# A two-layer encoder trunk: the Winograd steps of its MLPs in pairs that share operand quads, and a part of the QKV stage ordered by hand

## The chip, the core and the metric

One NeuronCore of a Trainium2 chip computes the whole trunk in one launch. Its engines run beside each other and wait for one another by semaphores: TensorE (PE) multiplies, VectorE (DVE), ScalarE (ACT) and GpSimd (POOL) work element by element, and transfers are issued from queues, here mostly those of SyncE (SP) and ScalarE. The metric is the device time of one execution in microseconds (us), lower is better.

## The reference

Everything is float32, 1024 tokens of width 1024. Layer 0 is a gated recurrent block, layer 1 chunked attention on keys and values that are computed once from layer 0's output. Each layer ends in an MLP of width 4096, and the change lies there and in the stage behind the first one:

```python
def sqrelu_mlp(hn, w1, w2):
    return jnp.square(jax.nn.relu(hn @ w1)) @ w2

def reference(...):
    for layer in range(DEPTH):          # DEPTH = 2
        ...                             # mixer of the layer, h = h + g1 * y
        hn = modulate(rms_norm(h, norm2_g[layer]), sh2, sc2)
        h = h + g2[:, None, :] * sqrelu_mlp(hn, mlp_w1[layer], mlp_w2[layer])
        if layer == N_A_LAYERS - 1:
            k_pad, v_pad = shared_kv(h, c_act, kv_norm_g, kv_ada_w, kv_ada_b, kv_w, k_norm_g)
    return h
```

Layer 1 begins with its own query projection from a norm of `h`, then the projection of the shared keys and values: the QKV stage.

## The kernel before

**Precision.** Every float32 operand is split into a high part (a rounding copy on ScalarE, L196) and a low part (what is left, a subtraction on VectorE, L200). `mm3` (L329 to L331) multiplies high by high, high by low and low by high: three matmuls, 128 by 128 by 512 columns, for each block product.

**Two products by Winograd's scheme.** Both matrix products of an MLP run in steps. A step takes a quad, two by two blocks of weights, and makes the four results with seven block products instead of eight (`PROD` lists them with their operand names B11, T1, T2, B22, B21, T3, T4 and the PSUM bank that each goes to). A block product is four times `mm3`, 12 matmuls. The sums of weight blocks are formed by four adds (`add_quad`, L126), those of the activations by four subtractions (L632 for the MLP's input, L1202 for the hidden layer). Banks are accumulated on: product 2 goes to the bank that product 0 began, 3 to that of 1, and 5 and 6 to that of 2, and after each product an engine reads what the bank holds into its place (`read`). So the next product on a bank must wait for the read of the one before. `Quads.step` runs products 0 to 5 of a step, with the last product (6) of the step before it between its second and third one (`late`).

**The first product** makes blocks p = 0 to 15 of the hidden layer: 0 and 1 by plain products, 2 to 15 by steps. ScalarE copies products 0 to 2 out of their banks (L1282), VectorE adds products 3 to 5 (L1284), ScalarE squares the positive part (L1213, L1214). `store` writes eight blocks for each p to `hid` in DRAM from ScalarE's queue: the four results first, then, when the sums are made, the four sums.

**The second product** makes steps s = 0 to 15 (layer 0: 0 to 14, and the last two output blocks by plain products on the extra weights `w2t`, so that the next norm can begin). Step s multiplies the quad of output blocks of s mod 4 with hidden blocks s to s+3, a window that moves on by one block each step; blocks 16 to 18 are 0 to 2 again, which the layout of `w2` allows for. Seven operand halves are therefore loaded and split for each step (`hid_item`, tile `ws`, split tiles `s`), but the first step needs four blocks at once, 28 operand tiles. VectorE adds each product from its bank to `h` (L1306), which `reload` brings back from the spilled copy `hsp` (L1271).

**The planner.** `Stream` holds one list of loads. Its clock `now` advances by one with each block product. After a product it issues what it may: loads up to `ns` raw tiles in flight (`load`, L159), splits up to a limit of live operands for weights (`w`, 8) and activations (`a`, `cap`), the quad sums (`p`) and the adaLN reductions (`u`, L362: rows of the modulation weights times the conditioning vector). Low parts are held back in `los` and flushed after the next product. All of layer 0 and the MLP of layer 1 stand in the order in which the code emits them (`manual_schedule`); the QKV stage and the attention are ordered by a scheduler. In the first product the quad sums go to VectorE, in the second, from step 2 on, to GpSimd (`G if s > 1 else V`).

## Time and profile before

| | before |
|---|---|
| median of 3 runs | 2332.1 us (2330.79 to 2334.56) |
| the profiled execution | 2332.22 us, span 2330.4 us, mean granted clock 0.994 |
| TensorE busy | 2248.5 us, 96% |
| VectorE, ScalarE, GpSimd busy | 1742.8, 1243.6 and 425.3 us |
| moved by DMA | 363.32 MB |
| layer 0's mixer; its MLP; QKV; attention; output projection and layer 1's MLP | about 0 to 480; to 1100; to 1370; to 1615; to 2330 us |

How to read the profile: a row of a group of instructions gives the line of the code, engine, operation, tiles written and read, sizes and count, then the busy time and mean duration in ns of one, then the idle time before them and what ended it. A row of the order of time gives start, duration, engine and the idle time just before in square brackets with the instruction that ended it. A row of a stretch gives the busy time of each engine in it, the clock granted to TensorE (1.00 is full speed), the mean busy share of the DMA engines and the rate. Matmuls overlap: of 512 columns each shows some 390 ns, while the next one starts earlier.

### The profile page before, as it was taken

What the parts mean: (1) busy time and instruction counts of PE and PEld (TensorE: products, weight loads), DVE (VectorE), ACT (ScalarE), POOL (GpSimd) and SP (SyncE); (2) the same over time, 40 slices, a digit from 0 to 9 for tenths busy, and PEclk for the clock granted to TensorE, in tenths of its full rate; (3) what the DMA queues carried; (4) which work ended last, traced back from release to release, by engine and by line L of the source; (5) the groups of instructions that cost most, each with busy time, mean ns of one, the idle gap of its engine ahead of it and who ended that gap; (6) DMA issues with size and microseconds to landing.
All of it is one profiled execution on the core that took longest, in us unless ns stands there. A gap on an engine that the chain in (4) does not pass through costs nothing. (4 is left out here: it accounts for less than half of the span.)

```text
span 2330.4 us, 29543 instructions
## 1 busy us (share of the span) xinstructions
PE 2248.5 (96%) x10588; PEld 1866.4 (80%) x10588; DVE 1742.8 (75%) x2560; ACT 1243.6 (53%) x2148; POOL 425.3 (18%) x439
## 2 busy tenths in 40 slices
PE   4999999999999899999999999999999999899999
PEld 2878878778888678888888889997888888678887
DVE  8579889698777887777777649995485556877775
ACT  5587793374555633344443259994375555633342
POOL 0001010200000033331000248863100000033332
PEclk9999999999999999999999999999999999999999
DMA  8225457426666855555344200024124444854444
GB/s 318 73 70 155 134 184 274 157 89 237 250 255 249 318 197 159 150 166 186 107 129 135 86 10 10 10 62 149 62 72 170 170 170 173 302 205 152 150 147 142
DMA packets 141631, 363.32 MB, mean 156 GB/s; under 512 B 14924, under 2 KB 17100, under 8 KB 141484
## 3 DMA queue, kind: packets, MB, share of 16 engines
q1 hardware_dynamic: 113756, 278.45, 35.4%
q10 hardware_dynamic: 23824, 71.44, 8.3%
q0 software_dynamic: 3904, 11.54, 1.9%
q8 instruction: 83, 1.36, 0.2%
q14 instruction: 64, 0.52, 0.1%
HBM read 260.19 MB, written 89.65 MB: 150 GB/s over the span
## 5 line engine op out<-in xcount | busy, mean ns | idle before, releaser
L329 PE MATMUL b<-s,wh 128*128 128x512 f32 (+1 forms) x2532 | 996.0, 393 | 22.8 <-DVE s L1306 7.0
L330 PE MATMUL b<-s,wh 128*128 128x512 f32 (+1 forms) x2532 | 992.3, 392 | 8.7 <-DVE s L825 5.3
L331 PE MATMUL b<-s,wl 128*128 128x512 f32 x2296 | 900.0, 392 | 8.8 <-DVE wl L200 8.8
L329 PEld LDWEIGHTS b<-s,wh 128*128 128x128 f32 (+1 forms) x2532 | 476.7, 188 | 132.3 <-ACT wh L196 9.1
L330 PEld LDWEIGHTS b<-s,wh 128*128 128x128 f32 (+1 forms) x2532 | 476.8, 188 | 115.5 <-DVE s L825 6.3
L196 ACT ACTIVATE wh<-ws 128x1024 fp32r<-128x1024 f32 (+3 forms) x302 | 291.6, 975 | 486.0 <-POOL ws L126 277.9
L331 PEld LDWEIGHTS b<-s,wl 128*128 128x128 f32 x2296 | 432.5, 188 | 103.4 <-DVE wl L200 10.5
L200 DVE TENSOR_TENSOR wl<-ws,wh 128x1024 fp32r<-128x1024 f32 (+1 forms) x249 | 305.3, 1228 | 86.5 <-ACT wh L196 82.7
L1306 DVE SCALAR_TENSOR_TENSOR s<-b,mod,s 128x512 f32<-128x512 f32 x221 | 164.9, 746 | 112.5 <-PE b L331 111.9
L200 DVE TENSOR_TENSOR s<-ws,s 128x512 fp32r<-128x512 f32 x284 | 221.3, 796 | 6.6 <-ACT s L196 6.6
L196 ACT ACTIVATE s<-ws 128x512 fp32r<-128x512 f32 x284 | 165.0, 618 | 76.9 <-DMA ws<-hid 39.1
L126 POOL TENSOR_TENSOR ws<-ws 128x512 f32<-128x512 f32 x21 | 28.7, 1368 | 954.7 <-DVE s L1306 375.3
L330 PE MATMUL b<-wl,s 128*128 128x512 f32 x384 | 149.9, 390 | 0.0
L329 PE MATMUL b<-wh,s 128*128 128x512 f32 x384 | 149.0, 389 | 0.0
L331 PE MATMUL b<-wh,s 128*128 128x512 f32 x384 | 146.5, 389 | 1.1 <-DVE s L593 1.1
L1284 DVE TENSOR_TENSOR s<-s,b 128x512 f32<-128x512 f32 x84 | 57.3, 684 | 107.5 <-PE b L331 96.2
L1282 ACT ACTIVATE s<-b 128x512 f32<-128x512 f32 x84 | 50.0, 595 | 92.5 <-PE b L331 92.4
L362 DVE CUSTOM_DVE_ANT_0 ws<-ws,cb,vec 128x1024 f32<-128x1024 f32 x59 | 75.0, 1278 | 31.7 <-DMA ws<-in_ada_dram 25.2
L331 PE MATMUL b<-s,wh 128*128 128x512 f32 x236 | 91.8, 389 | 0.0
L335 DVE TENSOR_TENSOR s<-b,s 128x384 fp32r<-128x384 f32 x144 | 82.6, 593 | 11.1 <-ACT s L334 10.6
L1598 POOL TENSOR_SCALAR s<-s,sm 128x640 f32<-128x640 f32 (+4 forms) x128 | 86.0, 684 | 22.4 <-DVE sm L1596 19.4
L1593 ACT ACTIVATE s<-s,sm 128x640 f32<-128x640 f32 (+4 forms) x128 | 88.3, 696 | 0.7 <-DVE sm L1591 0.7
(166 smaller groups left out, 2990.6 us busy)
## 6 DMA issues: line engine op xcount, KB each, us to landing
hid<-s ACTq DMA_DIRECT2D x128, 512.0 KB, 4.8
ws<-hid SPq DMA_DIRECT2D x118, 512.0 KB, 4.7
ws<-in_w_dram SPq DMA_DIRECT2D x220, 256.0 KB, 3.5
ws<-in_ada_dram SPq DMA_DIRECT2D x56, 512.0 KB, 4.6
s<-in_ada_dram SPq DMA_DIRECT2D x40, 512.0 KB, 8.2
ws<-in_w_in_dram SPq DMA_DIRECT2D x22, 512.0 KB, 7.4
hsp<-s SPq DMA_DIRECT2D x32, 256.0 KB, 2.0
s<-hsp SPq DMA_DIRECT2D x16, 512.0 KB, 7.2
```

The costliest lines, as they stand in the source:

```text
L196: self.nc.scalar.activation(out=hi[:rows, :n], in_=src, func=AF.Copy)
L200: self.nc.vector.tensor_tensor(out=lo[:rows, :n], in0=src, in1=hi[:rows, :n].bitcast(F32), op=ALU.subtract)
L329: PE.matmul(ps, ah, bh, start=start, stop=False, skip_group_check=more)
L330: PE.matmul(ps, ah, bl, start=False, stop=False, skip_group_check=more)
L331: return PE.matmul(ps, al, bh, start=False, stop=stop, skip_group_check=more).ins
L335: V.tensor_tensor(out=lo, in0=src, in1=hi.bitcast(F32), op=ALU.subtract)
L362: V.tensor_tensor_reduce(out=t, in0=t, in1=cb, op0=ALU.mult, op1=ALU.add, scale=1.0, scalar=bias, accum_out=dst)
L1282: A_.activation(out=t, in_=ps, func=AF.Copy)
L1284: V.tensor_tensor(out=t, in0=t, in1=ps, op=ALU.add)
L1306: V.scalar_tensor_tensor(out=t, in0=ps, scalar=g2[:, m : m + 1], in1=t, op0=ALU.mult, op1=ALU.add)
L1593: A_.activation(out=p[:, lo:640], in_=p[:, lo:640], func=AF.Exp, scale=-1.0, bias=m, accum_out=s1)
L1598: G.tensor_scalar(out=p[:, lo:640], in0=p[:, lo:640], scalar1=sm[:, 4 + e : 5 + e], scalar2=1.0, op0=ALU.mult, op1=ALU.mult)
```

## The change

1. `Quads.pair` runs two steps together: products 0 and 1 of the first, 0 and 1 of the second, 2 and 3 of each, 4 and 5 of each, then 6 of the first; 6 of the second waits for the next pair. Blocks 14 and 15 of the first product run so, and all steps of the second (layer 0's last, 14, alone).
2. In the second product steps 2t and 2t+1 share hidden blocks 2t to 2t+3. The window moves by two blocks every two steps; block 18 falls away. The weight layout follows (`w2`, `w2t`), and the planner's weight queue is interleaved (`interleave`).
3. Numbers of the planner: `ns` 10, then 11 raw tiles; `cap` for activations up to 24, growing from block 14 and 15's pair on; `strict`, by which all held-back low parts are emitted ahead of a quad sum on VectorE; another spread of the adaLN loads; other delays for the stores of blocks 12 to 15.
4. The quad sums of the second product are all on VectorE.
5. `store` writes the block that only layer 0's plain products use (B12) for p = 0, 1, 14, 15 of layer 0 alone, else 256 KB instead of 512 in that transfer.
6. The hand-set order ends later: the first group of the query projection is inside it, with `late_head` placing the second half's norm.

```diff
@@ Stream
+    def interleave(self, n):
+        q = self.queue["w"]
+        a, b = q[-n : -n // 2], q[-n // 2 :]
+        q[-n:] = [x for two in zip(a, b) for x in two]
@@ Stream.step
         if it["use"]:
+            if it["raw"] is None and self.strict and it["mine"]:
+                los, self.los = self.los, []
+                for low in los:
+                    low[2]()
@@ mlp_units
-            ada_late(0 if l or q == 2 else 2 if q in (3, 15) else 3)
-        for s in STEPS[: 16 if l else 15]:
-            def quad(s):
-                c = slice(s * 128, s * 128 + 512)
-                ws.add_quad(*(I["w2"][l][s % 4][x][:, c] for x in range(4)), 512,
-                            G if s > 1 else V)
...
+            ada_late(0 if l or q in (2, 14, 15) else 2 if q == 3 else 4 if q < 9 else 3)
+        ws.interleave(8)
+        def quad(s):
+            c = slice(s // 2 * 256, s // 2 * 256 + 512)
+            ws.add_quad(*(I["w2"][l][s % 4][x][:, c] for x in range(4)), 512, V)
+
+        def quads(t):
+            for s in range(2 * t, 2 * t + (2 if l or t < 7 else 1)):
+                quad(s)
+            if l or t < 7:
+                ws.interleave(8)
+
+        for nm in NAMES:
+            hid_item(l, [(0, nm), (1, nm)])
+            hid_item(l, [(2, nm), (3, nm)])
+            if nm == "B11":
+                quads(0)
+        for t in range(7):
+            for n, nm in enumerate(NAMES):
+                if n == 4:
+                    quads(t + 1)
+                hid_item(l, [(2 * t + 4, nm), (2 * t + 5, nm)])
@@ Quads
+        def pair(self, *two):
+            two = [(a[0], [bank(), bank(), None], *a[1:]) for a in two]
+            for x in (0, 2, 4):
+                for n, a in enumerate(two):
+                    if x == 4:
+                        a[1][2] = bank()
+                    self.product(x, *a)
+                    self.product(x + 1, *a)
+                    if x == 0 and n == 0:
+                        self.end()
+            self.product(6, *two[0])
+            self.late = two[1]
@@ mlp_body
-                nc.scalar.dma_start(hid[p][:, 0:8:7], ca.rearrange(f, a=2))
+                if l == 0 and p in (0, 1, 14, 15):
+                    nc.scalar.dma_start(hid[p][:, 0:8:7], ca.rearrange(f, a=2))
+                else:
+                    nc.scalar.dma_start(hid[p][:, 0:1], ca[:, hs(0)].unsqueeze(1))
...
-            for d, job in zip((2, 4, 13) if p == 14 else (6, 8, 13) if p == 15 else (2, 4, 8),
+            for d, job in zip({12: (2, 3, 4), 13: (2, 3, 4), 14: (2, 16, 20), 15: (6, 18, 22)}.get(p, (2, 4, 8)),
...
+        ws.strict = True
         quads = Quads()
-        for p in range(2, 16):
+        def hidden(p):
...
-                    ws.cap["a"] = 4 * x + 4
-                    if x == 3:
-                        reload(0, 1)
+                    ws.cap["a"] = min(24, 4 * x + 4)
+                    ws.ns = 10
+                    if x in (3, 5):
+                        reload(x - 3, x - 2)
+            return [ws.next() for _ in range(4)], 4, nrm.op, read, after
+
+        for p in range(2, 14):
+            quads.step(*hidden(p))
+        quads.pair(hidden(14), hidden(15))
...
+        for t in range(8):
+            if l or t < 7:
+                quads.pair(second(2 * t), second(2 * t + 1))
+            else:
+                quads.step(*second(2 * t))
@@ QKV
-    tokens(qt, n3, 0, 0, lambda k: head(k, n3))
+    def late_head(k):
+        if k == 1:
+            n3.mm(1)
+        elif k == 4:
+            n3.bc(1)
+            n3.mod(1, (0, 1, 2, 3))
+        elif k == 6:
+            n3.mod(1, (4, 5, 6, 7))
+
+    tokens(qt, n3, 0, 0, late_head)
+    order.close()
```

**How the order moves, at three places.** First SyncE's queue at layer 0's seam, where the first product ends and the second begins. `in_w_dram` stands for both weights, `hid` are operand loads, `hsp` the reload of `h`. Before, from the first operand load on:

```order
L159 DMA ws_5523<-hid 128x2x512
L159 DMA ws_5568<-hid 128x2x512
L159 DMA ws_5572<-in_w_dram 128x512
L159 DMA ws_5662<-in_w_dram 128x512
L159 DMA ws_5702<-in_w_dram 128x512 x2
L159 DMA ws_5707<-hid 128x2x512
L159 DMA ws_5735<-hid 128x2x512
L159 DMA ws_5741<-hid 128x2x512
L159 DMA ws_5769<-hid 128x2x512
```

After, from the same place:

```order
L163 DMA ws_5548<-hid 128x2x512
L163 DMA ws_5571<-hid 128x2x512
L163 DMA ws_5613<-in_w_dram 128x512
L163 DMA s_5648<-in_w_dram 128x512
L163 DMA s_5650<-in_w_dram 128x512 x2
L163 DMA s_5653<-in_w_dram 128x512
L163 DMA ws_5664<-in_w_dram 128x512
L163 DMA ws_5688<-in_w_dram 128x512 x2
L163 DMA ws_5734<-hid 128x2x512
L163 DMA ws_5738<-hid 128x2x512
L1293 DMA s_5770<-hsp_2446 128x1024
```

Two quads of weights instead of one are now loaded behind the first name's operands, some of them into tiles outside the ring `ws`, and the reload of `h` comes sooner, ahead of most operands.

Second the quad sums late in layer 1's second product. On GpSimd before, steps 13 and 14:

```order
L126 TENSOR_TENSOR ws_18791<-ws_18851 128x512
L126 TENSOR_TENSOR ws_18817<-ws_18851,ws_18791 128x512
L126 TENSOR_TENSOR ws_18795<-ws_18817,ws_18851 128x512
L126 TENSOR_TENSOR ws_18795<-ws_18817,ws_18795 128x512
L126 TENSOR_TENSOR ws_18943<-ws_19004 128x512
L126 TENSOR_TENSOR ws_18970<-ws_19004,ws_18943 128x512
```

On VectorE after, between bank reads (L1335), low parts (L208) and two sets of sums (L123) for the pair of steps 12 and 13:

```order
L208 TENSOR_TENSOR s_18612<-ws_18406,s_18612 128x512
L123 TENSOR_TENSOR ws_18505<-s_18552 128x512
L123 TENSOR_TENSOR ws_18530<-s_18552,ws_18505 128x512
L123 TENSOR_TENSOR ws_18509<-ws_18530,s_18552 128x512
L123 TENSOR_TENSOR ws_18509<-ws_18530,ws_18509 128x512
L1335 SCALAR_TENSOR_TENSOR s_17074<-b_18647,mod_83,s_17074 128x512
L208 TENSOR_TENSOR wl_18637<-ws_18505,wh_18636 128x1024
L208 TENSOR_TENSOR s_18639<-s_18429,s_18639 128x512
L208 TENSOR_TENSOR s_18643<-s_18429,s_18643 128x512
L1335 SCALAR_TENSOR_TENSOR s_17076<-b_18451,mod_83,s_17076 128x512
L1335 SCALAR_TENSOR_TENSOR s_17123<-b_18677,mod_83,s_17123 128x512
L123 TENSOR_TENSOR s_18557<-ws_18614 128x512
```

GpSimd has no sums left in the MLPs; on VectorE a set of four stands in one piece among the bank reads.

Third TensorE at the very end, before: the last rows of product 5 and the first of product 6, both on bank `b_19245`.

```order
L329 MATMUL b_19245<-s_19241,wh_19238 128x512
L330 MATMUL b_19245<-s_19241,wh_19238 128x512
L331 MATMUL b_19245<-s_19241,wl_19239 128x512
L329 MATMUL b_19245<-s_18815,wh_19243 128x512
L330 MATMUL b_19245<-s_18815,wh_19243 128x512
L331 MATMUL b_19245<-s_18815,wh_19243 128x512
```

After: the last rows of product 6 of the pair's first step, whose twelve matmuls are all on `b_19047`, and the first of the second step's product 6 on `b_19049`.

```order
L337 MATMUL b_19047<-s_19125,wh_19174 128x512
L338 MATMUL b_19047<-s_19125,wh_19174 128x512
L339 MATMUL b_19047<-s_19125,wh_19174 128x512
L337 MATMUL b_19049<-s_18848,wh_19176 128x512
L338 MATMUL b_19049<-s_18848,wh_19176 128x512
L339 MATMUL b_19049<-s_18848,wh_19176 128x512
```

A whole product now stands between the last two that go to one bank.

56 lines of the change are left out of this document (22 added, 34 removed).

## The prediction

> **What bounds the kernel now.** I read the page's busy times first, then the 60 us stretches of the whole span, then TensorE's own order of time where a stretch fell short, and last what the other engines and the queues did there. The page: engine, busy us, share of the span, instructions.
>
> ```profile
> PE 2248.5 (96%) x10588; PEld 1866.4 (80%) x10588; DVE 1742.8 (75%) x2560; ACT 1243.6 (53%) x2148; POOL 425.3 (18%) x439
> ```
>
> TensorE is the bound: the change can only win what TensorE stands idle or runs slowly. Stretches of 60 us (PE, PEld, DVE, ACT, POOL busy with instruction counts, then granted clock, DMA share, GB/s):
>
> ```profile
> 720.00:780.00 60.00, 60.00 (x266) 49.70 (x265) 48.10 (x70) 36.39 (x59) 0.00 (x0) 1.00 0.71 255
> 780.00:840.00 60.00, 50.34 (x205) 39.95 (x204) 51.29 (x70) 28.07 (x46) 6.57 (x4) 0.94 0.85 302
> 1920.00:1980.00 60.00, 60.00 (x267) 49.69 (x266) 34.92 (x47) 32.44 (x48) 0.00 (x0) 1.00 0.50 183
> 1980.00:2040.00 60.00, 51.98 (x216) 41.65 (x215) 51.36 (x75) 38.56 (x65) 0.00 (x0) 0.94 0.86 302
> 2040.00:2100.00 60.00, 57.31 (x246) 46.94 (x245) 48.48 (x57) 21.00 (x31) 18.78 (x12) 0.97 0.57 196
> 2100.00:2160.00 60.00, 60.00 (x267) 49.69 (x266) 46.00 (x58) 21.94 (x33) 19.01 (x12) 1.00 0.53 161
> ```
>
> Full stretches hold 266 matmuls of 512 columns, one per 0.2256 us, so a product of 12 takes 2.71 us and a step of seven 19.0. The three short stretches are the seams between the first and the second product, in layer 0 (780 on) and layer 1 (1980 on). TensorE's idle times there, the first three rows and 827.50 in layer 0, the next five in layer 1, then one after layer 0's last step; the row of waits is for 2065 to the end:
>
> ```profile
> 786.35 0.47 PE L329 MATMUL b<-s,wh 128*128 128x512 f32 x1 [2.78 <-DVE s L1306]
> 800.55 0.50 PE L329 MATMUL b<-s,wh 128*128 128x512 f32 x1 [2.79 <-ACT wh L196]
> 803.32 0.80 PE L331 MATMUL b<-s,wl 128*128 128x512 f32 x1 [2.03 <-DVE wl L200]
> ...
> 827.50 0.50 PE L331 MATMUL b<-s,wl 128*128 128x512 f32 x1 [2.03 <-DVE wl L200]
> 2011.83 0.47 PE L329 MATMUL b<-s,wh 128*128 128x512 f32 x1 [2.22 <-DVE s L1306]
> 2014.98 0.47 PE L329 MATMUL b<-s,wh 128*128 128x512 f32 x1 [0.17 <-DVE s L1306]
> 2026.98 0.50 PE L329 MATMUL b<-s,wh 128*128 128x512 f32 x1 [3.59 <-ACT wh L196]
> 2029.75 0.80 PE L331 MATMUL b<-s,wl 128*128 128x512 f32 x1 [2.03 <-DVE wl L200]
> 2054.11 0.50 PE L331 MATMUL b<-s,wl 128*128 128x512 f32 x1 [2.69 <-DVE wl L200]
> 1075.83 0.47 PE L329 MATMUL b<-s,wh 128*128 128x512 f32 x1 [0.94 <-DVE s L1306]
> 1128.89 1.21 PE L331 MATMUL b<-wh,s 128*128 128x512 f32 x4 [1.10 <-DVE s L593]
> PE b L329 <- DVE s L1306: 0.9, 1, 0.9
> ```
>
> The seams' waits are 2.78+2.79+2.03+2.03 = 9.63 us in layer 0 and 2.22+0.17+3.59+2.03+2.69 = 10.70 in layer 1. The releasers are splits of weights and adds on VectorE, but these were late themselves; stretches of 5 us show why (the same columns, DMA share and GB/s last):
>
> ```profile
> 780.00:785.00 5.00, 3.57 (x16) 2.63 (x14) 4.90 (x9) 3.11 (x7) 0.00 (x0) 1.00 1.02 387
> 785.00:790.00 5.00, 3.62 (x15) 2.77 (x16) 5.00 (x8) 4.35 (x8) 0.00 (x0) 1.00 1.05 388
> 790.00:795.00 5.00, 5.00 (x24) 4.14 (x23) 5.00 (x9) 4.94 (x10) 0.00 (x0) 1.00 1.03 388
> ...
> 800.00:805.00 5.00, 2.42 (x6) 1.70 (x7) 4.93 (x8) 4.52 (x8) 0.00 (x0) 0.75 0.75 288
> 805.00:810.00 5.00, 5.00 (x14) 3.92 (x14) 3.27 (x5) 0.59 (x2) 0.00 (x0) 0.56 1.02 328
> 810.00:815.00 5.00, 5.00 (x24) 4.13 (x23) 3.25 (x6) 1.79 (x3) 0.00 (x0) 1.00 1.04 399
> 2025.00:2030.00 5.00, 0.98 (x3) 0.55 (x4) 4.78 (x7) 3.65 (x5) 0.00 (x0) 0.79 0.71 260
> 2030.00:2035.00 5.00, 5.00 (x13) 3.94 (x14) 3.27 (x5) 2.02 (x4) 0.00 (x0) 0.53 1.00 321
> 2055.00:2060.00 5.00, 5.00 (x17) 3.93 (x16) 4.15 (x6) 1.63 (x3) 0.00 (x0) 0.66 0.91 309
> ```
>
> Two things are to be seen: the DMA engines are full at 387 to 399 GB/s while VectorE is full too, and behind a pair of waits TensorE computes at about half clock. That half clock costs, as busy time times the missing share, 2.42x0.25 + 5x0.44 = 2.81 us in layer 0 and 0.98x0.21 + 5x0.47 + 5x0.34 = 4.26 in layer 1.
>
> **The change, part by part.** All sums are made against the profiled execution, 2332.2 us beside a span of 2330.4; the median of the three runs, 2332.1, is the same number.
>
> (1) TensorE's work: the same 10,238 rows of matmuls. Cost 0.
>
> (2) The seams. Counted from the planner, product by product: before, the eight products ahead of the second product carry 12.06 MB of loads and stores, 554 GB/s over 8x2.71 us, against 399 that the row shows. The 28 operand tiles of one quad set (four blocks, seven names) are used up in seven products. Now 14 products share them, and the last 11 products ahead of the second product with its first three carry 15.2 MB (layer 0: 15.5) in 14x2.71 = 37.9 us, 401 to 408 GB/s: still full, but the transfers needed last are used 14 products after the seam, not seven. The slack tells more than the rate: before, a weight's VectorE split stands two to five products ahead of its first use and a hid operand's four to five; now four to six and five to nine. One product of slack is 2.71 us and the longest wait above is 3.59. A second bank effect goes with it: a PSUM bank is read by VectorE (L1306) and accumulated on again; a step leaves two products between these, a pair at least two and mostly three or four, which covers the 2.78 and 2.22. So I cost the seams at no wait: -9.63 -10.70, and with them the half clock, -2.81 -4.26. The cover is this slack; if it is gone, the next thing late is the split of the second weight of pair (0,1) or a hid operand behind ScalarE, which now queues eight half-tile splits at a time behind loads. Bounds: nothing is left, or all of it stays; the row nearest to one left wait is 2.03 to 2.79 us plus 1.7 to 2.8 of half clock, so 4 to 5.5 each. I take none.
>
> The half clock's length has a second source. The Trainium skill, "TensorE: Matmul & The Clock Gate", Part 1, says that an idle window of about 3.4 us halves the clock and some 3.4 us of work restores it. By that, as an estimate, three such stretches would cost 3x1.7 = 5.1 us and the forecast would be 2.0 us higher; the rows show half clock after waits of 2.69 us and for more than 5 us, and they decide.
>
> (3) The sums of w2's quads go from GpSimd to VectorE, 108 instructions. Rows of VectorE's hid splits in the second product (2100 to 2280 us) and at layer 1's seam (1985 to 2065, hardly any GpSimd beside them), of its adds in the first product (1740 to 1980), of GpSimd's adds (2100 to 2280), and of the adaLN reductions (the page); the number behind the comma is ns of one:
>
> ```profile
> L200 DVE TENSOR_TENSOR s<-ws,s 128x512 fp32r<-128x512 f32 x65 | 56.1, 863 | 0.0
> L200 DVE TENSOR_TENSOR s<-ws,s 128x512 fp32r<-128x512 f32 x43 | 27.8, 683 | 2.8 <-ACT s L196 2.8
> L126 DVE TENSOR_TENSOR ws<-ws,ws 128x512 f32<-128x512 f32 x39 | 26.9, 690 | 0.9
> L126 POOL TENSOR_TENSOR ws<-ws,ws 128x512 f32<-128x512 f32 x17 | 26.6, 1567 | 0.8
> L362 DVE CUSTOM_DVE_ANT_0 ws<-ws,cb,vec 128x1024 f32<-128x1024 f32 x59 | 75.0, 1278 | 31.7 <-DMA ws<-in_ada_dram 25.2
> ```
>
> VectorE is busy 46.0 of 60 us there, 14.6 per step. Four adds more are 4x0.69 = +2.8; the seven hid splits should fall from 863 to 683 ns without GpSimd beside them, -1.3. That makes 16.1 of 19.0 us: hidden beside TensorE, with 2.9 us per step to spare. Cost 0, and above that only what passes 19.0 (rival D); a gain is excluded while TensorE is full there. Queued behind the adds are the bank reads of L1306; the largest heap that the plan builds is under one product. Nine splits fewer (block 18 isn't loaded) on ScalarE and VectorE, and less stored for hid (28 stores of 256 KB instead of 512): hidden before and now, 0. In layer 0 four adaLN reductions per step in place of three in the early blocks: one more is the 1.28 us of the row of L362, on an engine with 48.10 of 60 us busy at 720; 0.
>
> (4) QKV by hand. The 1.10 us at 1128.89 is a norm's low part (L593) late for the second half; the parts that this half needs first are now issued after the fifth of eight k, 36 matmuls or 8.1 us ahead of it. -1.10. ScalarE and VectorE also have the next weights' splits and adaLN sums in hand-set order there, whose loads can block VectorE; behind them stand only that group's reductions. Bounds +2.8 (the longest wait on such an add) to -1.10; I take -1.10, since the weights' splits stand ahead of the reductions.
>
> (5) The end of layer 1: the last product accumulates on the bank of the product just before it, 0.9 us. In a pair another step's product lies between: -0.9. The 0.94 at 1075.83 is the same in layer 0, whose last step stays single: 0.
>
> Sum: 9.63+10.70+2.81+4.26+1.10+0.9 = 29.4, and 2332.2 - 29.4 = 2302.8 us. A check by counts: the three short stretches lack 61+50+20 = 131 matmuls, 29.6 us, against 27.4 here; the higher one would give 2300.6, some of it records missing at the edges.
>
> **The rivals.**
>
> The seams run dry again (B). For it: the loads of the pair still come to 401 GB/s or more, and 3.7 MB of them are issued behind one product, two before the seam. Against it: slack of four to nine products. About half of the seam's loss stays: 2332.2 - 2.0 - 27.4/2 = 2316.5. The Trainium skill, "DMA: Bandwidth & Descriptors", Specifications, speaks for it with a limit of about 358 GB/s of HBM per core; the rows' 387 to 399 go past it.
>
> The waits only move (C): pair (0,1) starts clean and the second or third pair waits for loads that the burst pushed back, with the same price; 2332, no change. Against it: the plan has the queues empty again five products after the seam.
>
> VectorE becomes the bound in the second product (D, slower). Place: 31 steps. If the adds on VectorE take GpSimd's 1.57 us and the splits stay at 863, a step is 14.6+6.3 = 20.9 us, 1.9 over; 2332.2 - 29.4 + 31x1.9 gives 2361.7. It decides from 0.95 us over a step, 20.0 us of VectorE work. Against it: the same adds took 690 ns there in the first product.
>
> **How the numbers follow.** A measurement of this kernel (runs within 0.16% of each other) tells about 0.2%, 4.7 us. Forecast 0.72 (2300 to 2306); B 0.15 (2306 to 2322); C 0.04; D 0.05; 0.04 for a slower case not named. Faster by over 0.2%: forecast and B, 0.87; within: C, 0.04; slower: D and the rest, 0.09. The range takes the forecast and the lower half of B: 2300 to 2314.
>
> **What would show it.** In the changed profile the stretches at both seams should hold 265 or so matmuls in 60 us at clock 1.00, with no TensorE idle over 1 us; VectorE in the second product some 84% busy with hid splits near 690 ns and GpSimd at 0; L593 no longer a releaser; 0.9 us left only after layer 0. Wrong it would be with a wait on L204's splits (L196 before) or a half clock left at a seam, or TensorE waiting for VectorE in every step.

## The result, and the profile after

The changed kernel takes 2314.8 us (median of 4 runs, 2313.5 to 2315.7) beside 2331.4 for the kernel before on the same chip: a ratio of 0.9927, with a 95% interval of 0.9909 to 0.9944. That is 16.6 us, 0.73%, where 29.4 us had been forecast. The profiled execution took 2313.97 us with a span of 2312.2, so 11.2 us of the forecast's sum are missing in it. The page's busy times:

```profile
PE 2242.3 (97%) x10588; PEld 1862.5 (81%) x10588; DVE 1761.7 (76%) x2658; ACT 1241.0 (54%) x2138; POOL 256.2 (11%) x331
```

The 60 us stretches at both seams and three of the second product (the columns are those shown before):

```profile
720.00:780.00 60.00, 57.77 (x255) 47.48 (x254) 39.68 (x55) 30.14 (x48) 0.00 (x0) 1.00 0.56 198
780.00:840.00 60.00, 58.61 (x258) 47.97 (x257) 53.88 (x77) 34.76 (x56) 0.00 (x0) 1.00 0.84 297
1980.00:2040.00 60.00, 55.89 (x244) 45.31 (x243) 50.74 (x75) 35.34 (x58) 0.00 (x0) 1.00 0.86 303
2040.00:2100.00 60.00, 59.94 (x265) 49.33 (x264) 55.59 (x79) 26.94 (x39) 0.00 (x0) 1.00 0.63 206
2100.00:2160.00 60.00, 60.00 (x266) 49.67 (x266) 51.08 (x73) 23.17 (x34) 0.00 (x0) 1.00 0.48 150
2160.00:2220.00 60.00, 60.00 (x267) 49.67 (x266) 47.99 (x68) 22.44 (x36) 0.00 (x0) 1.00 0.48 152
2220.00:2280.00 60.00, 60.00 (x266) 49.71 (x265) 49.63 (x69) 24.48 (x38) 0.00 (x0) 1.00 0.48 155
```

In this execution the half clock is gone at the seams (1.00 in each row). It is not gone in every one: the profile of experiment 2 below, whose order is the same from block 14 on, has a clock of 0.66 from 775 to 780 us and from 820 to 825, and of 0.73 from 2040 to 2045. VectorE in the second product is at 148.7 of 180 us (the last three rows), where TensorE is busy throughout. But the stretch ahead of layer 0's seam, which was full before, lacks 2.2 us, and 1980 to 2040 still lacks 4.1. TensorE's idle times in its order of time, all of 0.25 us and more that stand in the MLPs behind 600 us:

```profile
630.13 0.50 PE L337 MATMUL b<-s,wh 128*128 128x512 f32 x1 [1.43 <-DVE s L1308]
776.81 0.50 PE L337 MATMUL b<-s,wh 128*128 128x512 f32 x1 [2.23 <-DVE s L1308]
799.87 0.47 PE L337 MATMUL b<-s,wh 128*128 128x512 f32 x1 [0.97 <-DVE s L1335]
816.86 0.47 PE L337 MATMUL b<-s,wh 128*128 128x512 f32 x1 [0.42 <-DVE s L1335]
855.50 0.47 PE L337 MATMUL b<-s,wh 128*128 128x512 f32 x1 [0.29 <-DVE s L1335]
1069.43 0.50 PE L337 MATMUL b<-s,wh 128*128 128x512 f32 x1 [1.49 <-DVE s L1335]
1994.81 0.50 PE L337 MATMUL b<-s,wh 128*128 128x512 f32 x1 [1.93 <-DVE s L1308]
2018.06 0.47 PE L337 MATMUL b<-s,wh 128*128 128x512 f32 x1 [1.15 <-DVE s L1335]
2035.67 0.47 PE L337 MATMUL b<-s,wh 128*128 128x512 f32 x1 [1.03 <-DVE s L1335]
```

Not one of these waits is for an operand. All are for a PSUM bank that VectorE has not yet read (L1308 in the first product, L1335 in the second, L1284 and L1306 before), while before six of the nine at the seams were for a weight's split (L196 or L200). With the 1.49 counted against the 0.94 that stood there before, they are 10.0 us. Most of the rest is half clock in a place that the change does not touch, the start of layer 1's output projection (at 1594.5 us here, at 1601.9 before). Behind the same wait of 2.0 us TensorE ran at a mean clock of 0.72 over 5 us after the change, and at full clock before it. The first row is of after, the second of before:

```profile
1595.00:1600.00 5.00, 5.00 (x17) 3.95 (x17) 0.00 (x0) 0.00 (x0) 3.08 (x2) 0.72 1.01 409
```

```profile
1600.00:1605.00 5.00, 3.10 (x14) 2.57 (x15) 1.81 (x2) 0.50 (x1) 2.91 (x2) 1.00 0.78 270
```

5.00 x 0.28 is 1.4 us, and the stretch ahead of it (2.96 us busy at 0.94) adds 0.2. So 10.0 + 1.6 = 11.6 stands against the 11.2 missing. The 1.6 is chance and not the change's doing: in the profile of experiment 3, which runs the same code there, TensorE keeps full clock behind the same 2.03 us.

**How a bank read comes late.** The wait of 2.23 us at 776.81, followed back: SyncE's own queue (SPq), ScalarE and VectorE in order of time. First what SyncE waited for between 752 and 780 us (in total, times, longest), then the three engines:

```profile
SPq L163 <- DVE wh L208: 13.7, 1, 13.7
```

```profile
768.59 1.28 DVE L208 TENSOR_TENSOR wh<-ws,wh 128x512 fp32r<-128x512 f32 x2
769.30 0.98 SPq L163 DMA_DIRECT2D ws<-hid  x2
774.20 1.15 ACT L204 ACTIVATE s<-ws 128x512 fp32r<-128x512 f32 x2 [5.89 <-DMA ws<-hid]
774.86 1.29 DVE L208 TENSOR_TENSOR s<-ws,s 128x512 fp32r<-128x512 f32 x2 [2.65 <-ACT s L204]
776.07 0.68 DVE L1308 TENSOR_TENSOR s<-s,b 128x512 f32<-128x512 f32 x1
```

The load of two hid operands stood in SyncE's queue for 13.7 us, until VectorE's low part of a weight (L208) freed its tile at 769.3. The plan counts a raw tile as free when its high part is issued, one product earlier, though the low part still reads it. The transfer took 4.9 us (769.30 to 774.20). ScalarE had the split queued two products after the planned load and stood 5.89 us; VectorE's low part stood 2.65 us behind it, and the bank read (L1308) behind that. The operand itself is for the second product, whose first bank read is at 790.90: it is only its place in two in-order queues that made TensorE wait.

Behind the seam the set of sums plays this part. In the second experiment below, whose order is the same from block 14 on, VectorE stood 4.73 us at the first add, and TensorE 4.26 at the bank behind it:

```profile
813.31 0.69 DVE L123 TENSOR_TENSOR s<-ws 128x512 f32<-128x512 f32 x1 [4.73 <-DMA ws<-in_w_dram]
819.86 0.47 PE L337 MATMUL b<-s,wh 128*128 128x512 f32 x1 [4.26 <-DVE s L1335]
```

In the changed kernel's own profile the same set does not stand at all, and yet 0.42 us are lost:

```profile
810.32 0.68 DVE L123 TENSOR_TENSOR s<-ws 128x512 f32<-128x512 f32 x1
815.97 2.06 DVE L1335 SCALAR_TENSOR_TENSOR s<-b,mod,s 128x512 f32<-128x512 f32 x3
```

VectorE works almost without a pause from 804.7 to 818 us there. Two low parts and the set (809.12 to 812.97, 3.85 us) stand ahead of one bank read, and three low parts (813.63 to 815.97) ahead of the next three. So a read can come late in two ways: something ahead of it waits for a transfer, or what stands ahead of it is simply long.

### The profile page after: what moved, and what is told of

Its sections match the earlier page's. It is cut to its first block, busy times and chain, and to the rows that moved or that the text cites. A ratio compares the mean times of both kernels' runs of the same rounds, so it can differ in the third digit from the quotient of the medians.

```text
span 2312.2 us, 29207 instructions
## 1 busy us (share of the span) xinstructions
PE 2242.3 (97%) x10588; PEld 1862.5 (81%) x10588; DVE 1761.7 (76%) x2658; ACT 1241.0 (54%) x2138; POOL 256.2 (11%) x331
## 5 line engine op out<-in xcount | busy, mean ns | idle before, releaser
L204 ACT ACTIVATE wh<-ws 128x1024 fp32r<-128x1024 f32 (+3 forms) x264 | 253.0, 971 | 348.2 <-PE b L338 152.9
L208 DVE TENSOR_TENSOR wl<-ws,wh 128x1024 fp32r<-128x1024 f32 (+1 forms) x216 | 262.8, 1220 | 65.6 <-ACT wh L204 61.8
L1335 DVE SCALAR_TENSOR_TENSOR s<-b,mod,s 128x512 f32<-128x512 f32 x221 | 163.4, 746 | 88.5 <-PE b L339 88.5
L204 ACT ACTIVATE s<-ws 128x512 fp32r<-128x512 f32 x196 | 112.3, 620 | 57.5 <-DMA ws<-ygd 17.5
L1308 DVE TENSOR_TENSOR s<-s,b 128x512 f32<-128x512 f32 x84 | 57.0, 683 | 102.6 <-PE b L339 102.5
L208 DVE TENSOR_TENSOR s<-ws,s 128x512 fp32r<-128x512 f32 x196 | 125.2, 683 | 7.6 <-ACT s L204 7.5
L204 ACT ACTIVATE wh<-s 128x1024 fp32r<-128x1024 f32 (+1 forms) x52 | 50.4, 969 | 144.5 <-issue 45.9
L1573 POOL TENSOR_SCALAR dk<-s 128x1024 f32<-128x1024 f32 x16 | 18.6, 1162 | 833.2 <-DVE s L1513 830.6
L1306 ACT ACTIVATE s<-b 128x512 f32<-128x512 f32 x84 | 50.0, 595 | 87.7 <-PE b L339 87.1
```

What stands on the lines that cost most here:

```text
L204: self.nc.scalar.activation(out=hi[:rows, :n], in_=src, func=AF.Copy)
L208: self.nc.vector.tensor_tensor(out=lo[:rows, :n], in0=src, in1=hi[:rows, :n].bitcast(F32), op=ALU.subtract)
L1306: A_.activation(out=t, in_=ps, func=AF.Copy)
L1308: V.tensor_tensor(out=t, in0=t, in1=ps, op=ALU.add)
L1335: V.scalar_tensor_tensor(out=t, in0=ps, scalar=g2[:, m : m + 1], in1=t, op0=ALU.mult, op1=ALU.add)
```

## The experiments

Two theories stood against each other. Theory Q: what is left is VectorE's order, bank reads behind low parts and sums whose operand has not landed. The rivals: VectorE is overloaded by the sums (S, V), or the DMA engines are full and everything is late (B, F, T). Further letters are explained where an expectation brings them in. All ratios are to the kernel before, run on the same chip, with the 95% interval in square brackets; 0.001 is 2.3 us. The changed kernel stands at 0.9927. Where code lines are left out of a diff stands `...`.

**1. The sums on GpSimd again.**

```diff
-            ws.add_quad(*(I["w2"][l][s % 4][x][:, c] for x in range(4)), 512, V)
+            ws.add_quad(*(I["w2"][l][s % 4][x][:, c] for x in range(4)), 512, G if s > 1 else V)
```

> The changed kernel with one thing undone: the sums of w2's quads from step 2 on are formed on GpSimd again. Theory Q (what is left at the seams is VectorE's order: a bank read, L1308 or L1335, stands in its queue behind low parts whose operand came late): only the waits ahead of which a set of four sums stands on VectorE go, 0.42 and 0.29 us in layer 0 (816.86 and 855.50) and 1.03 in layer 1 (2035.67), 1.7 us together; the 2.23, 0.97, 1.93 and 1.15 stay, since steps 0 and 1 have their sums on VectorE in both. About 2313 us. Rival S (VectorE is overloaded by the sums as a whole): all waits on L1335 go, 0.97+0.42+0.29+0.55+1.15+1.03 = 4.4 us, about 2310. Rival D (the sums are late on GpSimd, 4 x 1.57 = 6.3 us instead of 2.8, and slow VectorE's splits to some 860 ns): new waits of 2 us and more behind the seam, 2317 or above.

Measured: 2329.1 us, 0.9983 [0.9974, 0.9992]. Nearly the whole gain is lost, as rival D had it. TensorE's waits behind the seams (layer 0's two, layer 1's two), and VectorE beside GpSimd's adds at 853.8:

```profile
816.11 0.47 PE L337 MATMUL b<-s,wh 128*128 128x512 f32 x1 [2.72 <-DVE s L1335]
858.05 0.47 PE L337 MATMUL b<-s,wh 128*128 128x512 f32 x1 [3.60 <-DVE s L1335]
2042.76 0.47 PE L337 MATMUL b<-s,wh 128*128 128x512 f32 x1 [3.83 <-DVE s L1335]
2085.72 0.47 PE L337 MATMUL b<-s,wh 128*128 128x512 f32 x1 [2.98 <-DVE s L1335]
...
853.80 3.45 DVE L208 TENSOR_TENSOR s<-s,s 128x512 fp32r<-128x512 f32 x2
857.17 2.06 DVE L1335 SCALAR_TENSOR_TENSOR s<-b,mod,s 128x512 f32<-128x512 f32 x3
```

Two low parts took 3.45 us there, against 1.28 for such a pair elsewhere, and three bank reads had queued up behind them: the reads again, by another road. The pair needs two sets of sums in a short stretch, and GpSimd, at 1.3 to 2.2 us an add in this profile, both is late and slows VectorE's splits. So the sums' move, costed at 0, is what lets the pairs work: it is worth some 13 us to them. Theories Q and S both missed this.

**2. adaLN spread evenly.**

```diff
-            ada_late(0 if l or q in (2, 14, 15) else 2 if q == 3 else 4 if q < 9 else 3)
+            ada_late(0 if l or q in (2, 14, 15) else 4 if q in (5, 7, 9, 11) else 3)
```

> The changed kernel with the 37 adaLN loads of layer 0's first product spread evenly over blocks 3 to 13 (3 each, 4 in blocks 5, 7, 9 and 11) instead of four each in blocks 4 to 8. If the four per step are what made the wait of 1.43 us at 630.13 (SyncE's queue held by adaLN loads, so that a weight of w1 came late), it is gone and the time falls by 1.4, to about 2313; the 2.23 us at 776.81 stays. Rival: any step with four holds the queue, then one to four waits of 0.5 to 1.5 us appear in blocks 5 to 11 and the time stays at 2314.8 or rises to 2317.

Measured: 2314.8 us (2313.4 to 2321.3), 0.9929 [0.9915, 0.9943]. The 1.43 us at 630 did not appear. But it did not appear in experiments 1 and 3 either, which keep four loads in blocks 4 to 8, and one of 1.44 us at 649 came back in a later run with the old spread. So it is a wait that comes and goes with the transfers, and the spread is not shown to be its cause. This profile had the 4.26 us at 819.86 shown above, where the changed kernel's had 0.42: the same instructions behind the same transfer, which had landed in time in one execution and not in the other.

**3. Splits of activations three products after their load, from block 15 until the second product begins.**

```diff
-                    ws.lag["p"] = 2
+                    ws.lag["p"], ws.lag["a"] = 2, 3
...
-                    ws.lag["p"] = 4
+                    ws.lag["p"], ws.lag["a"] = 4, 2
```

> The changed kernel with one number changed: from block 15 on, until the second product begins, an activation's high part is issued three products after its load instead of two. Theory Q: the waits of 2.23 us (layer 0, 776.81) and 1.93 us (layer 1, 1994.81) come from a split on ScalarE that is queued 5.4 us after a load which starts late, because its tile is not free before VectorE's low part of a weight is done; with 2.7 us more both waits fall below 0.5 and the time falls by 3.5 to 4, to about 2311. Price: operands come 2.7 us later, so 0.97 and 1.15 may grow by up to 1 us each. Rival F (the DMA engines are full at the seam and every operand is late by that): the waits move to the next product with the same 4 us, 2314 to 2316.

Measured: 2308.0 us, 0.9900 [0.9886, 0.9913]. The stretches that held the two waits are full (the second was part of 1980 to 2040):

```profile
720.00:780.00 60.00, 60.00 (x266) 49.69 (x265) 40.84 (x56) 32.83 (x52) 0.00 (x0) 1.00 0.59 215
1960.00:2020.00 60.00, 60.00 (x267) 49.67 (x266) 48.11 (x69) 39.46 (x65) 0.00 (x0) 1.00 0.82 291
```

Both waits are gone; rival F falls for the part ahead of the seam. Theory Q had forecast 2311, and a price at the 0.97 and 1.15; instead these two are gone from the profile as well. Left are waits behind sets of sums:

```profile
812.05 0.47 PE L337 MATMUL b<-s,wh 128*128 128x512 f32 x1 [1.43 <-DVE s L1335]
851.16 0.47 PE L337 MATMUL b<-s,wh 128*128 128x512 f32 x1 [0.75 <-DVE s L1335]
2026.76 0.47 PE L337 MATMUL b<-s,wh 128*128 128x512 f32 x1 [0.56 <-DVE s L1335]
2067.15 0.47 PE L337 MATMUL b<-s,wh 128*128 128x512 f32 x1 [2.03 <-DVE s L1335]
```

**4. The kernel before with the QKV part alone** (the hand-set order ends later, with `late_head`).

> The kernel before with part 6 of the change alone: the first group of the query projection in hand-set order, the second half's norm after the fifth k. The prediction's term: the 1.10 us at 1128.89 goes and nothing else moves, ratio 0.9995, 1.1 us. Rival: the hand-set order costs a wait of 0.5 to 2.8 us elsewhere in the first 30 us of that stage, ratio 1.000 to 1.001.

Measured: 2330.7 us beside 2333.4, 0.9990 [0.9982, 0.9999]. The wait for L593 is not in its profile and no other came in its stage. The 1.1 us lies in the interval.

**5. As 3, and all sums five products after their load instead of four.**

```diff
-                    ws.lag["p"], ws.lag["a"] = 4, 2
+                    ws.lag["p"], ws.lag["a"] = 5, 2
```

> The kernel of the third experiment (activations' splits three products after their load at the seam), and the sums of w2's quads five products after their load instead of four. Its profile left 1.43 us in layer 0 (812.05) and 0.56 in layer 1 (2026.76) behind a set of sums that waited on VectorE for a transfer of w2 (0.52 us in one run, 4.73 in another of the same order). Theory Q (queue order: sums issued before their transfer has landed hold the bank reads behind them): with 2.7 us more these two waits go, and the same place no longer varies between runs; about 2 us less than the third experiment, ratio about 0.989. Rival V (VectorE has no room there, busy 15 of 15 us from 800 to 815): the wait only moves one product on, ratio 0.990 as before. Rival L (the second step's weights are now split too late, two products ahead of their use instead of three): new waits of 1 to 3 us for L204 or L208, ratio 0.991 to 0.993.

Measured: 2318.3 us, 0.9939 [0.9926, 0.9952], slower than 3. The waits at the sums went, as Q had it, and rival L came: the second set's weights were split just too late, in both layers, with half clock behind (0.69 and 0.63 in the ten us from 825).

```profile
825.09 0.50 PE L337 MATMUL b<-s,wh 128*128 128x512 f32 x1 [1.10 <-ACT wh L204]
827.84 0.79 PE L339 MATMUL b<-s,wl 128*128 128x512 f32 x1 [2.03 <-DVE wl L208]
```

**6. As 3, and the last block's hid sums eight products later.**

```diff
-            for d, job in zip({12: (2, 3, 4), 13: (2, 3, 4), 14: (2, 16, 20), 15: (6, 18, 22)}.get(p, (2, 4, 8)),
+            for d, job in zip({12: (2, 3, 4), 13: (2, 3, 4), 14: (2, 16, 20), 15: (6, 26, 30)}.get(p, (2, 4, 8)),
```

> The kernel of the third experiment, with the last block's hid sums (L1224, four on VectorE) 26 products after its end instead of 18. Theory V (local overload: in the third pair two sets of w2's sums and the hid sums, 12 x 0.69 = 8.3 us, stand within 14 products on VectorE): the waits of 0.75 us at 851.16 and 2.03 at 2067.15, behind which VectorE had no idle time for 15 us, go: about 2.5 us less, ratio about 0.989. Rival: the two sets of sums alone fill VectorE there, then 0.75 and 2.03 stay within 0.5 us and the ratio stays at 0.990.

Measured: 2306.6 us, 0.9892 [0.9879, 0.9905]. The stretch with the 2.03 us, first of experiment 3, then of this one:

```profile
2040.00:2100.00 60.00, 57.97 (x256) 47.69 (x255) 55.07 (x80) 22.70 (x34) 0.00 (x0) 1.00 0.66 214
```

```profile
2040.00:2100.00 60.00, 60.00 (x266) 49.71 (x265) 56.29 (x81) 26.19 (x38) 0.00 (x0) 1.00 0.63 210
```

VectorE is as busy in both. Theory V holds: twelve VectorE instructions in one heap were too many, and eight products' distance was enough. It is local order, not the share. The 0.75 at 851 went too. What remains in this profile is 3.00 us at 814.09 and 1.31 at 2033.08, behind the second pair's first set of sums, which stood 1.82 us for its transfer in layer 0. The gain in time over experiment 3 is within the intervals.

**7. The sums done twice in the steady part.**

```diff
-                                      (x1[:, b], x2[:, b], x1[:, a], ALU.subtract)):
+                                      (x1[:, b], x2[:, b], x1[:, a], ALU.subtract)) * times:
...
-            ws.add_quad(*(I["w2"][l][s % 4][x][:, c] for x in range(4)), 512, V)
+            ws.add_quad(*(I["w2"][l][s % 4][x][:, c] for x in range(4)), 512, V,
+                        2 if s > 5 else 1)
```

> The changed kernel with each of the four adds of w2's sums done twice (the same values again) from step 6 on, in the steady part of the second product: 4 x 0.69 = 2.8 us of VectorE more per step, in layer 0 nine steps and in layer 1 ten. By the prediction's sum VectorE has 16.1 of 19.0 us per step, so with 18.9 it is just not the bound: below 2 us more in all, about 2316. By theory Q the share does not decide but the length of what stands in one piece ahead of a bank read: a set of 5.6 us plus the low parts that follow outlasts the two products between a bank's last matmul and its next use, so TensorE waits 1 to 3 us at most of the sets: 10 to 40 us more, 2325 to 2355, with TensorE's waits on L1335 behind runs of L123.

Measured: 2324.7 us, 0.9963 [0.9950, 0.9975]. Two of the steady waits, which recur every 38.57 us, and a stretch:

```profile
897.25 0.47 PE L337 MATMUL b<-s,wh 128*128 128x512 f32 x1 [0.23 <-DVE s L1336]
935.82 0.47 PE L337 MATMUL b<-s,wh 128*128 128x512 f32 x1 [0.22 <-DVE s L1336]
...
2160.00:2220.00 60.00, 59.56 (x262) 48.70 (x262) 57.48 (x83) 24.88 (x37) 0.00 (x0) 1.00 0.49 158
```

A pair takes 38.57 us instead of 38.08 (961.04 to 999.12 between two like sets in the changed kernel), 0.49 more, or some 4.7 us over nine pairs and a half. So the prediction's sum of VectorE's time was good: with 2.8 us more per step it sits just at the edge. The 1 to 3 us per set of theory Q were too many. The rest of the 8 us is not in the doubled part. In this profile the waits at the seams, ahead of it, are larger than in the changed kernel's (3.85 us at 818.65, 2.66 at 2044.25), like those of experiment 2. Why they are large in most runs of this kernel is not shown.

**8. Blocks 14 and 15 of the first product one after the other.**

```diff
-        ws.interleave(8)
...
-        for p in range(2, 14):
+        for p in range(2, 16):
             quads.step(*hidden(p))
-        quads.pair(hidden(14), hidden(15))
```

> The changed kernel with blocks 14 and 15 of the first product run one after the other again (and their weights not interleaved); all else as changed, the second product in pairs. If what the change won at the seams comes from the first product's pair (it lets the operands' loads start four products earlier), the seams' waits of 2 to 3 us with half clock come back in part: 2320 to 2328. If it comes from the second product's pairs alone (14 products that share 28 operand tiles), the time stays within 3 us of 2314.8.

Measured: 2309.5 us (2308.5 to 2315.0), 0.9905 [0.9891, 0.9919]. Neither expectation held: it is some 5 us faster than the changed kernel, near the edge of what the two intervals can tell. The first product's pair brings nothing here; the waits of 2.23 and 1.93 are its own, and without it they are 0.58 and 0.59 (for L1305, the copies on ScalarE). Its profile, of the slowest of its four runs, has one of 2.46 us at 745.64 that no other profile shows, a bank read behind hid sums that waited 2.58 us for a store, and one of 2.25 at 2018.75. What the change gains at the seams does not need the first product's pair. It comes from the second product's pairs together with the planner's numbers (part 3 of the change), which no run undoes as a whole.

**9. As 6, and the reload of h's last four blocks behind the second pair's weights.**

```diff
-                if x == 3 and s < 2:
+                if (s, x) in ((0, 4), (1, 5)):
                     reload(4 + 2 * s, 5 + 2 * s)
```

> The kernel of the experiment with the later hid sums, with the reload of h's last four blocks moved: blocks 4 and 5 after product 4 of step 0 instead of product 3, blocks 6 and 7 after product 5 of step 1 instead of product 3 of it, so behind the loads of the second pair's w2 on SyncE's queue and not between them. What is left at 812 to 820 us (0.42 to 4.26 in the runs so far) and at 2027 to 2041 (0.56 to 2.78) is a set of sums that holds VectorE until w2's transfer lands. Theory T (that transfer shares full DMA engines, 390 to 411 GB/s, with 2 MB of h): both waits fall below 0.5 in each run, the spread between runs shrinks, ratio 0.987 to 0.988. Rival (w2's loads are issued late because their tile is freed late by VectorE): the waits stay between 0.5 and 3, ratio 0.989.

Measured: 2316.2 us, 0.9923 [0.9910, 0.9937], slower than 6, and the waits stayed: 3.53 us at 817.85 and 2.30 at 2036.62. Theory T falls. SyncE's waits in this run from 790 to 819 us show what held all but the first of w2's loads until 803.4:

```profile
SPq L163 <- DVE s L208: 11.7, 6, 4.8
```

Tiles came free late, behind VectorE's low parts, as the rival had it. The five loads of hid operands ahead, 2.6 MB, already filled the DMA engines (a share of 0.94 to 1.05 in each 5 us from 785 to 805). Why the whole is slower than 6 is not shown.

**10. The full stores again.**

```diff
-                if l == 0 and p in (0, 1, 14, 15):
+                if True:
```

> The changed kernel with part 5 undone: B12 of every block is stored again, 512 KB instead of 256 in 28 transfers, 7.3 MB more. The prediction's term is 0: these stores run from 560 to 780 and from 1740 to 1980 us, where the DMA engines are 0.40 to 0.70 busy; 2314 to 2316. Rival (transfers that ScalarE issues delay the operands' loads at the seam): 2 to 4 us more, 2317 to 2319, in the waits of 776 and 1994.

Measured: 2318.3 us, 0.9930 [0.9916, 0.9943] beside 0.9927: no difference that can be told. In its profile the wait ahead of layer 1's seam is 3.25 us instead of 1.93 and the one in layer 0 2.43 instead of 2.23, so an effect of a microsecond or two as the rival had it is not excluded.

**11. Experiment 8 with 6's and 9's edits.**

> Blocks 14 and 15 of the first product one after the other as in the experiment on that, with the last block's hid sums later (26 instead of 18 products) and the reload of h's last four blocks behind the second pair's w2, but splits two products after the load as in the changed kernel. By the sum of parts: 2309.5 less 0.4 to 2 in layer 0 and 2 in layer 1, about 2306, ratio 0.988, beside 0.988 for the paired version with the later splits. If the first product's pair is worth anything once its splits are late enough, this one is behind the paired version by 2 us or more.

Measured: 2312.5 us (2307.6 to 2316.7), 0.9906 [0.9890, 0.9923]. Nothing over experiment 8, as 9 would lead one to think. It is 3 to 4 us behind the paired versions of 6 and 13, but the intervals overlap and 9's edit is in it, so what the first product's pair is worth with later splits stays open.

**12. The kernel before with the sums on VectorE alone.**

```diff
-                            G if s > 1 else V)
+                            V)
```

> The kernel before with part 4 of the change alone: all sums of w2's quads on VectorE. The prediction's term: hidden beside TensorE, 0, with hid splits at some 690 ns instead of 863; ratio 0.999 to 1.001. Theory Q: in the old order a set of four stands ahead of a bank read that is due two products later; 2.8 us and a low part are under 5.4, so 0 here too, but at the seams, where VectorE is full, 1 to 3 us more: 1.000 to 1.002. Rival (the change's gain of the seams is in truth the sums' move): 3 us or more faster, below 0.9985.

Measured: 2333.5 us, 0.9996 [0.9987, 1.0004]. In the old order the move is worth nothing, as predicted; in the new one 13 us (experiment 1). The parts do not add up: the sums' place is a condition of the pairs.

**13. As 6, and the first of the second pair's two sets of sums one product later.**

```diff
                 if (s, x) == (0, 0):
-                    ws.lag["p"], ws.lag["a"] = 4, 2
+                    ws.lag["p"], ws.lag["a"] = 5, 2
+                if (s, x) == (0, 4):
+                    ws.lag["p"] = 4
```

> The kernel with the later splits and the later hid sums, and the first of the second pair's two sets of sums five products after its load instead of four (the second set stays at four, so that its weights are split when they were). Theory Q: this set is emitted ahead of a bank read although its transfer, issued at 800 to 805 us and 5 to 8 us long, has not landed; one product later the read passes first, and the waits at 812 to 820 (3.00 in the last profile of that order) and 2033 (1.31) fall below 1 in sum; ratio 0.987 to 0.988, with a smaller spread between runs. Rival B (all operands there are late because the DMA engines are full): the next read or split waits instead, ratio 0.989 or above.

Measured: 2306.8 us (2305.6 to 2307.5), 0.9889 [0.9872, 0.9905]. The waits at the sums are gone from both layers in its profile. What is left behind the seams is this in layer 0, and 0.34 in layer 1:

```profile
797.22 0.47 PE L337 MATMUL b<-s,wh 128*128 128x512 f32 x1 [0.72 <-DVE s L1335]
798.26 0.50 PE L339 MATMUL b<-s,wl 128*128 128x512 f32 x1 [0.34 <-DVE wl L208]
```

The ratio is that of 6 within the intervals, and the spread between runs is the smallest, 1.8 us. This version beats both the kernel before and the changed one (0.9927, whose interval begins at 0.9909), and so does that of 6.

**14. The changed kernel without the reload of h.** GpSimd sets the blocks to zero instead; the output lacks that term.

```diff
                 h[k] = slot()
-                nc.sync.dma_start(h[k], nrm.dram[k])
+                G.memset(h[k], 0.0)
```

> The changed kernel without the reload of h: the eight blocks are set to zero by GpSimd instead of loaded from DRAM, so that 4.2 MB of the 15.2 MB that cross each seam are gone; the output lacks that term and only the time is read. Theory Q (planned order: a split or a set of sums is queued on ScalarE or VectorE before its tile can be free and its load issued): the waits of 1.9 to 2.2 us at 776 and 1994 stay within 0.7, those at 800 to 820 and 2018 to 2041 fall by half at most; about 2311. Rival B (the full DMA engines are the cause of all): all six waits fall below 0.5, 8 us less, about 2306.

Measured: 2310.1 us, 0.9906 [0.9891, 0.9920]. The waits that were 2.23, 0.97, 0.42, 0.29 in layer 0 and 1.93, 1.15, 1.03 in layer 1 (layer 0 has only the first one left):

```profile
775.91 0.50 PE L337 MATMUL b<-s,wh 128*128 128x512 f32 x1 [2.25 <-DVE s L1308]
1994.43 0.50 PE L337 MATMUL b<-s,wh 128*128 128x512 f32 x1 [0.55 <-DVE s L1308]
2016.64 0.47 PE L337 MATMUL b<-s,wh 128*128 128x512 f32 x1 [0.16 <-DVE s L1335]
2033.90 0.47 PE L337 MATMUL b<-s,wh 128*128 128x512 f32 x1 [0.66 <-DVE s L1335]
```

The time is Q's, but neither theory holds everywhere. Ahead of layer 0's seam the planned order alone makes the wait: it stays with 4.2 MB taken out. Ahead of layer 1's, 1.93 us fall to 0.55, and behind the seams 3.86 fall to 0.82, more than Q allowed: there the reload makes the operands late, and VectorE's order hands it on to TensorE. The edit also takes the reload's issues out of SyncE's queue, and which of the two counts, the bytes or the places in the queue, is not told apart.

## Why the prediction was wrong, point by point

**What bounds the kernel, (1) TensorE's work:** right. The page counts 10588 TensorE instructions before and after (the prediction's 10,238 is in none of the rows shown), and the time moved with TensorE's idle time and its clock.

**(2) The seams: this is the step that failed.** Its first half held: with slack of four to nine products no operand's split releases a wait in the changed kernel, where 3.59 and 2.79 us stood before. The half clock (2.81 and 4.26) went in the profiled execution, but that is in part luck, since waits of some 2 us were left that bring it back in others. (Its 554 GB/s should be 556; nothing hangs on that.) The failure is in the sentence on banks: that two to four products between the accumulations on a bank cover its read, "so I cost the seams at no wait". It set those products against the old waits (2.78 and 2.22), and not against what the new order puts ahead of the read in VectorE's queue. The seams kept 2.23+0.97+0.42+0.29 and 1.93+1.15+1.03, 8.0 us, where 0 was put. Experiments 3, 6 and 13, each built on the one before, removed all but 1.4 us of these in the last profile by later emission of the split or the sums, with the same transfers. The part named as next in line, a hid operand behind ScalarE, was the right culprit ahead of the seam; only its victim was a bank read and not a matmul that uses it.

**(3) The sums on VectorE:** the steady sum was right: hid splits at 684 ns for 683, VectorE at 148.7 of 180 us or 15.7 of each 19.0 for 16.1, and twice the adds cost 0.49 us per pair. Two statements were wrong. "The largest heap that the plan builds is under one product" leaves out the wait for a transfer ahead of the set, 4.73 us in one run, and even its work was 3.85 us (809.12 to 812.97) against the 2.71 of a product. And costing the part by itself at 0 hid that the pairs fail without it (experiment 1 against 12). The stores: 0 as far as the runs can tell (experiment 10); the splits saved are tried in no run. The four adaLN loads per step: 0 as far as the runs can tell; the 1.43 us at 630 was not in the sum and comes and goes.

**(4) QKV:** right; the 1.10 us is gone, and alone it gave 0.9990 [0.9982, 0.9999].

**(5) The end of layer 1:** right, the 0.94 is gone. After layer 0's last step 1.49 us stand where 0.94 stood. That was costed at 0. In the trace the read that releases TensorE there (1068.63) stands behind a weight's low part which VectorE began at 1067.50, so it is the same failure; no run moves that low part.

**The rivals.** B gave 2316.5, close to the result, and that nearness is partly luck: B halved the old waits and half clock for dry DMA queues, while in experiment 14 about half of the 8.0 us (4.4) goes with the reload of h. No rival had the bank read behind VectorE's in-order queue, through which all of these waits reach TensorE, whether the queue stands for a transfer or is only long. C and D did not happen; by experiment 7 D's edge is about where it was put.

The half clock of some 1.6 us at 1595, outside the change, is the last piece of the 11.2.

## What to carry to other kernels

When operands get more slack, ask for each split and each sum what is queued behind it on its in-order engine: an instruction that is emitted before its transfer has landed passes its wait to every PSUM read behind it, and TensorE pays for a bank although its operands are ready. A heap of work longer than the products between two uses of a bank does the same without any wait. A planner's lag has to be counted from when the load can start, which is when the last reader of its tile is done (here VectorE's low part, one product after the high part). And a part that prices at 0 alone can be the condition of another: undo it in the new kernel as well as adding it to the old one.

## What the runs showed of the hardware

Half clock behind a wait of some 2 us is not a fixed price. At the same place, behind waits of 2.23 and 2.25 us, TensorE kept full clock in the changed kernel (first row) and ran at 0.68 in experiment 14 (second):

```profile
775.00:780.00 5.00, 3.19 (x14) 2.62 (x15) 3.55 (x6) 4.75 (x9) 0.00 (x0) 1.00 0.93 335
```

```profile
775.00:780.00 5.00, 4.08 (x11) 3.23 (x12) 3.61 (x6) 4.94 (x10) 0.00 (x0) 0.68 0.67 190
```

In stretches of 1 us from 776 on the clock of experiment 14 is 0.91, 0.50, 0.50, 0.50 and 0.89. So the half clock lasted some 3.4 us, and its price was 0 in the one execution and 0.09+0.50+0.50+0.50+0.11 = 1.7 us in the other. The 1.7 to 2.8 of the prediction are one outcome, and a removed wait of 2 us is worth 2 to 4 us. The Trainium skill, "TensorE: Matmul & The Clock Gate", Part 1, says that the activity window is free-running, so that the moment of the transition depends on where in it the first matmul lands. The two rows fit that. It puts the idle time needed for half clock at one window or more, of about 3.4 us each, and these rows show half clock after 2.25; the measurement decides.

VectorE's two-input splits from SBUF slow down beside GpSimd's adds, 3.45 us for two against 1.28, while its bank reads, with one input in PSUM, do not: over 2100 to 2280 us they average 745 ns in experiment 1 (first row) and 747 in the changed kernel (second).

```profile
L1335 DVE SCALAR_TENSOR_TENSOR s<-b,mod,s 128x512 f32<-128x512 f32 x67 | 49.5, 745 | 36.1 <-PE b L339 36.1
```

```profile
L1335 DVE SCALAR_TENSOR_TENSOR s<-b,mod,s 128x512 f32<-128x512 f32 x66 | 48.9, 747 | 30.6 <-PE b L339 30.6
```

The Trainium skill, "SBUF — State Buffer", Who interferes with whom, has this rule: a VectorE instruction with two SBUF inputs contends with a GpSimd instruction that reads SBUF, one with at most one SBUF input does not. Both rows and the 3.45 us agree.
